# Queries' and keys' norm in an encoder kernel: the root moves beside the turning, gains multiplied straight from PSUM, query transposes and casts in two steps

## The chip, the cores and the metric

The kernel runs on one core of a Trainium2 chip. The metric is the time of one execution in device microseconds (us), median of several runs. The engines are called by the profile's names: PE (TensorE, matmuls and transposes), DVE (VectorE), ACT (ScalarE), POOL (GpSimd) and SP (which only issues DMAs here). Each engine works through its own instructions in program order, and waits where an input or a buffer isn't ready.

## The reference

Two layers of an encoder over 768 tokens (sequences of 256 and 512), width 1024. Each layer normalises its input, projects it, runs three branches side by side (windowed attention, a bidirectional mLSTM, a bidirectional state-space branch, called SSD) and merges them. The change touches the queries and keys of the attention:

```python
def rms_norm(x, g):
    y = xf * lax.rsqrt(jnp.mean(xf * xf, axis=-1, keepdims=True) + RMS_EPS)
    return (y * g.astype(jnp.float32)).astype(x.dtype)

def partial_rope(x, pos):            # turns the first 16 of a head's 64 channels
    x1 = x[..., :half]
    x2 = x[..., half:ROT_DIM]
    return jnp.concatenate([x1 * cos - x2 * sin, x2 * cos + x1 * sin, x[..., ROT_DIM:]], axis=-1)
...
proj = h @ w_in
...
aq = partial_rope(rms_norm(aq.reshape(bsz, s_len, ATT_HEADS, ATT_HEAD_DIM), q_norm_g), pos)
ak = partial_rope(rms_norm(ak.reshape(bsz, s_len, ATT_KV_HEADS, ATT_HEAD_DIM), k_norm_g), pos)
```

There are 8 query heads and 2 key heads of 64 channels.

## The kernel before

**Work and tiles.** The 768 tokens are six tiles of 128. Every fp32 operand of a large matmul is kept as two parts, a high part (rounded to the matmul's format, by an ACT cast) and a low part (the rest, by a subtraction), and a product takes three matmuls. `H` holds the normalised input in this form, transposed; `R` is an arena of such pairs, with four weight slots; `F` is an arena of plain fp32. Each layer begins with the queries (`aq`): for each tile 24 matmuls of 512 columns. Then come keys, values and gates (`akv`, 24 matmuls of 288 columns a tile), then column blocks of the other projections (128x512 and 128x256 matmuls), with the branches' own work in between. At a layer's end item `W` multiplies by the output weights, tile by tile, 48 matmuls each; its first tile needs all of `H` and eight weight pieces. In layer 0 item `W` is followed by the next layer's norm and transposes.

**Weights.** A piece of at most 128x1024 lands by DMA in a raw slot of `F`. `split_w` casts the high part on ACT, then writes the low part (`lo`) on DVE or on POOL, whichever a cost rule says would be done first; then the raw slot is free, and SP issues the next piece into it.

**The norm of a query tile** (`qk_norm`, then `q_put`). The 128x512 result stands in a PSUM bank. Before the change: ACT squares it and copies it to `F`; DVE sums the squares per head (TENSOR_REDUCE, 128x8); POOL takes the inverse root (`rstd`: TENSOR_SCALAR, then a power on 128x8); DVE multiplies by the root and then by the gains; POOL turns 16 channels of each head in four small operations; PE transposes the tile (4 transposes of 128x128); ACT casts the high part in four pieces of 64x256, DVE subtracts the low part in four. A key tile does the same with 128 columns. Tiles use three buffers in turn.

**What sets the order.** The program is written out by a planner: each chain of work (a "task") is a generator, and each `yield` ends a step. The planner has a clock model (`Clock`: a cost for each instruction, and `HOP`, the time from one engine to the next) and puts a step into the program where the model says that its inputs are ready, between groups of about six projection matmuls. So a number in the model changes where the transposes stand among the matmuls. Nothing is reordered at run time.

All engine instructions go through one helper, so they have one line, 316, in the profile; they are told apart by shapes and tiles. Line numbers below are those of the kernel before.

Of the kernel before, what the change touches and what calls it, by code (L numbers as in the profile page):

```python
# [32 lines left out]
TOK = 768  # L33
# [131 lines left out]


# [40 lines left out]
class Clock:  # L207
# [4 lines left out]
    HOP = 180.0  # L212
# [56 lines left out]
    def note(self, eng, cost, outs, ins):  # L269
        code, t, same = self.ENG[eng], 0.0 if eng == "dma" else self.free[eng], self.SAME[eng]  # L270
        acc = []
        for aps, write in ((ins, False), (outs, True)):
            for ap in aps:
                m = self.mem.get(ap.tensor.name)
                if m is None:
                    continue
                for sl in self.spans(ap):
                    acc.append((m, sl, write))
                    t = max(t, (m[0][sl] + np.where(m[1][sl] != code, self.HOP, same)).max())
                    if write:  # L280
                        t = max(t, (m[2][sl] + self.HOP * (m[3][sl] != code)).max())
        shared = eng in ("dve", "pool") and self.two(ins)
        if shared:
            t = max(t, self.port)
# [116 lines left out]
class Body:  # L401
# [295 lines left out]
    def split_w(self, slot, t, hi, lo):  # L697
        self.nc.scalar.copy(hi, t)
        yield

        at = {e: max(self.clk.free[e], self.now) + c for e, c in (("dve", 1.1 * t.shape[1]), ("pool", 2.3 * t.shape[1]))}
        g = self.nc.vector if at["dve"] <= at["pool"] else self.nc.gpsimd
        g.tensor_tensor(out=lo, in0=t, in1=hi.bitcast(F32), op=ALU.subtract)
        self.raw_back(slot)
# [183 lines left out]
    def aq_begin(self, l, _):  # L888
        s = self.S[l]
        self.finish(s["consts"])  # L890
        for g in range(2):
            s["q", g] = self.R.alloc(4 * TOK)
        s["k"] = self.R.alloc(4 * TOK)
        s["qkr"] = Ring(self.F, 3, 1024)
# [13 lines left out]
    def qk_norm(self, l, i, p, nh, goff, t):  # L908

        s, nc = self.S[l], self.nc  # L910
        st = s["qks"].next()
        n = 64 * nh
        t1, t2 = t[:, 0:n], t[:, 512:512 + n]
        a3 = t1.rearrange("p (h d) -> p h d", h=nh)
        b3 = t2.rearrange("p (h d) -> p h d", h=nh)
        nc.scalar.activation(out=t2, in_=p[:, 0:n], func=AF.Square)
# [15 lines left out]
        gp.tensor_tensor(out=b3[:, :, 0:8], in0=a3[:, :, 8:16], in1=sn0, op=ALU.mult)  # L932
        gp.tensor_tensor(out=b3[:, :, 8:16], in0=a3[:, :, 0:8], in1=sn1, op=ALU.mult)
        gp.tensor_tensor(out=a3[:, :, 0:16], in0=a3[:, :, 0:16], in1=cos, op=ALU.mult)
        gp.tensor_tensor(out=a3[:, :, 0:16], in0=a3[:, :, 0:16], in1=b3[:, :, 0:16], op=ALU.add)

    def q_put(self, l, i, p, t):
# [7 lines left out]
        parts = [(self.S[l]["q", g].ap.rearrange("p (j e t) -> p j e t", j=2, e=2),  # L945
                  b[:, 256 * g:256 * g + 256].rearrange("p (j t) -> p j t", j=2)) for g in range(2)]
# [4 lines left out]
        for q4, b3 in parts:  # L951
            for e in range(2):
                nc.vector.tensor_tensor(out=q4[half[1 - e], :, e, ts], in0=b3[half[e]], in1=q4[half[e], :, e, ts].bitcast(F32),
                                        op=ALU.subtract)
# [958 lines left out]
```

## Time and profile before

| what | value |
|---|---|
| time, median of 3 runs | 1718.99 us (1718.66 to 1720.11) |
| the profiled execution, its own time | 1719.23 us |
| its span, first to last instruction | 1717.4 us |
| mean granted TensorE clock | 0.994 of full speed |
| PE busy | 1678.1 us, 98% of the span |
| DVE busy | 916.6 us, 53% |
| ACT busy | 642.7 us, 37% |
| POOL busy | 333.5 us, 19% |
| PE's share of the chain that ended last | 87% |

The span is the time from the first instruction to the last; the run's own time has 1.8 us more around it. An engine's idle time is told with what ended it, "[1.13 <-POOL F L316]" meaning 1.13 us idle until a POOL instruction that wrote tile `F` was done. The granted clock is that at which PE was allowed to run: 1.00 is 2.4 GHz and 0.50 is 1.2 GHz.

### The profile page before, as it was taken

How to read it: one execution, taken by the hardware profiler on the slowest of the kernel's cores; microseconds unless marked ns; L12 is line 12 of the kernel's file. 1: busy time of each engine (PE TensorE's matmuls, PEld its weight loads, DVE VectorE, ACT ScalarE, POOL GpSimd, SP SyncE). 2: the span in 40 equal slices, each digit the busy share in tenths (PEclk: the TensorE clock that was granted, in tenths of full speed). 3: DMA queues.
4: the chain of work that ended last, by engine and by line, in shares of the span. 5: the costliest groups of instructions: out<-in, count | busy, mean ns of one | idle time of the engine just before them, and what ended most of it. 6: DMA issues, size and time to landing. Idle time of an engine off the chain costs nothing.

```text
span 1717.4 us, 25480 instructions
## 1 busy us (share of the span) xinstructions
PE 1678.1 (98%) x9902; PEld 1440.5 (84%) x9902; DVE 916.6 (53%) x2121; ACT 642.7 (37%) x1425; POOL 333.5 (19%) x411
## 2 busy tenths in 40 slices
PE   8899999999999999999998999999999999999999
PEld 6788888888888888888877887898888878888877
DVE  6665456454484972246346645564445859623441
ACT  5446653232332532233135466532223345222310
POOL 4513320000003112014035223100000031301230
PEclk9999999999999999999999999999999999999999
DMA  5101032321114532234211101222121145331522
GB/s 200 62 27 38 25 99 65 98 68 62 68 62 122 196 128 81 79 136 157 99 44 61 53 26 50 75 77 99 68 71 59 58 152 190 105 111 41 172 86 74
DMA packets 47881, 152.18 MB, mean 89 GB/s; under 512 B 5616, under 2 KB 6544, under 8 KB 47760
## 3 DMA queue, kind: packets, MB, share of 16 engines
q1 hardware_dynamic: 47760, 150.55, 26.1%
q8 instruction: 78, 1.28, 0.3%
q14 instruction: 43, 0.35, 0.1%
HBM read 131.51 MB, written 19.02 MB: 88 GB/s over the span
## 4 chain that ended last, share of the span: by engine, by line
PE 87%; DVE 6%; ACT 2%; POOL 2%; DMA 1%; issue 1%; SPq 0%; ACTq 0%; POOLq 0%; DVEq 0%
PE psum L316 87%; DVE F L316 3%; DVE R L316 2%; POOL F L316 2%; ACT R L316 1%; ACT F L316 1%; DMA F<-wts_dram 1%; DMA F<-csd 1%; DMA F<-cstb_dram 0%; POOL R L316 0%; SPq L316 0%; DVE H L316 0%; ACT H L316 0%; ACTq L316 0%; POOLq L316 0%
## 5 line engine op out<-in xcount | busy, mean ns | idle before, releaser
L316 PE MATMUL psum<-H,R 128*128 128x512 f32 x4800 | 889.7, 341 | 0.5 <-DVE R L316 0.5
L316 PEld LDWEIGHTS psum<-H,R 128*128 128x128 f32 x4800 | 734.7, 189 | 109.5 <-issue 7.8
L316 PE MATMUL psum<-R,H 128*128 128x512 f32 (+2 forms) x1752 | 392.2, 379 | 8.1 <-DVE R L316 4.8
L316 PEld LDWEIGHTS psum<-R,H 128*128 128x128 f32 x1752 | 310.7, 191 | 66.0 <-DVE R L316 7.4
L316 DVE TENSOR_TENSOR R<-F,R 128x1024 fp32r<-128x1024 f32 (+3 forms) x163 | 206.6, 1278 | 243.6 <-ACT R L316 242.0
L316 DVE SCALAR_TENSOR_TENSOR F<-F 128x128 f32<-128x128 f32 (+5 forms) x596 | 251.2, 469 | 76.9 <-POOL F L316 35.3
L316 POOL TENSOR_TENSOR F<-F 128x32 f32<-128x32 f32 (+9 forms) x216 | 202.4, 946 | 441.7 <-DVE F L316 243.2
L316 ACT ACTIVATE F<-F 128x128 f32<-128x128 f32 (+8 forms) x432 | 201.8, 495 | 230.6 <-DVE F L316 219.5
L316 PE MATMUL psum<-F 128*128 128x128 f32 (+5 forms) x2006 | 247.7, 287 | 27.4 <-POOL F L316 16.5
L316 PEld LDWEIGHTS psum<-F 128*128 128x128 f32 (+2 forms) x2006 | 202.3, 163 | 67.3 <-POOL F L316 21.2
L316 PE MATMUL psum<-R 128*128 128x512 f32 (+2 forms) x1344 | 247.1, 336 | 0.0
L316 ACT CAST R<-F 128x1024 fp32r<-128x1024 f32 (+3 forms) x226 | 195.0, 875 | 100.7 <-DVE F L316 50.9
L316 PEld LDWEIGHTS psum<-R 128*128 128x128 f32 x1344 | 204.2, 189 | 30.6 <-issue 2.1
L316 ACT ACTIVATE F<-psum 128x768 f32<-128x768 f32 (+2 forms) x124 | 89.0, 718 | 344.1 <-PE psum L316 276.7
L316 POOL TENSOR_SCALAR F<-F 128x256 f32<-128x256 f32 (+7 forms) x112 | 70.4, 633 | 531.4 <-ACT F L316 334.6
L316 ACT COPY F<-psum 128x256 f32<-128x256 f32 (+7 forms) x286 | 105.2, 402 | 175.9 <-PE psum L316 174.4
L316 DVE SCALAR_TENSOR_TENSOR F<-F,psum 128x768 f32<-128x768 f32 (+3 forms) x124 | 88.6, 725 | 91.1 <-PE psum L316 48.1
L316 DVE SCALAR_TENSOR_TENSOR F<-psum,F 128x128 f32<-128x128 f32 (+4 forms) x75 | 37.5, 505 | 176.9 <-PE psum L316 165.6
L316 POOL TENSOR_TENSOR R<-F,R 128x128 fp32r<-128x128 f32 (+1 forms) x63 | 60.1, 957 | 318.2 <-ACT R L316 294.0
L316 DVE TENSOR_TENSOR F<-F 128x2 f32<-128x2 f32 (+8 forms) x340 | 100.2, 305 | 32.8 <-ACT F L316 20.6
L316 DVE TENSOR_SCALAR F<-F 128x128 f32<-128x128 f32 (+5 forms) x230 | 67.4, 322 | 45.9 <-ACT F L316 22.1
L316 DVE TENSOR_TENSOR R<-psum,R 64x256 fp32r<-64x256 f32 (+2 forms) x72 | 33.5, 466 | 47.6 <-ACT R L316 46.8
(24 smaller groups left out, 282.8 us busy)
## 6 DMA issues: line engine op xcount, KB each, us to landing
F<-wts_dram SPq DMA_DIRECT2D x164, 512.0 KB, 3.6
mg<-F SPq DMA_DIRECT2D x32, 384.0 KB, 3.0
F<-mg SPq DMA_DIRECT2D x32, 384.0 KB, 4.2
F<-csd SPq DMA_DIRECT2D x32, 384.0 KB, 5.4
F<-x_dram SPq DMA_DIRECT2D x12, 512.0 KB, 7.6
F<-md SPq DMA_DIRECT2D x16, 384.0 KB, 5.5
x<-F SPq DMA_DIRECT2D x6, 512.0 KB, 2.9
F<-x SPq DMA_DIRECT2D x6, 512.0 KB, 4.0
```

The source lines that it names most:

```text
L316: r = fn(*args, **kw)
```

## The change

In `qk_norm` ACT no longer copies the tile out of PSUM. DVE multiplies it by the gains straight from PSUM into `F`, POOL turns it at once (the turning is linear and leaves the root's factor alone), DVE sums the squares meanwhile, POOL takes the root, and DVE multiplies by the root last. In `q_put` the transposes are a step of their own, the casts another, and the two blocks of queries become one of double size, so that two casts of 64x512 and two subtractions take the place of four and four. The clock model has 250 ns after PE and 170 ns after any other engine in place of 180, and the rule in `split_w` adds 2000 ns to POOL's price.

```diff
     GRAIN = 4
-    HOP = 180.0
+    HOP = 170.0
+
+    HOPS = np.array([0.0, 250.0, 170.0, 170.0, 170.0, 170.0])
...
-                    t = max(t, (m[0][sl] + np.where(m[1][sl] != code, self.HOP, same)).max())
+                    t = max(t, (m[0][sl] + np.where(m[1][sl] != code, self.HOPS[m[1][sl]], same)).max())
...
-        at = {e: max(self.clk.free[e], self.now) + c for e, c in (("dve", 1.1 * t.shape[1]), ("pool", 2.3 * t.shape[1]))}
+        at = {e: max(self.clk.free[e], self.now) + c for e, c in (("dve", 1.1 * t.shape[1]), ("pool", 2.3 * t.shape[1] + 2000.0))}
...
         nc.scalar.activation(out=t2, in_=p[:, 0:n], func=AF.Square)
-        nc.scalar.copy(t1, p[:, 0:n])
+        nc.vector.tensor_tensor(out=a3, in0=p[:, 0:n].rearrange("p (h d) -> p h d", h=nh),
+                                in1=s["cb"][:, goff:goff + 64].unsqueeze(1).to_broadcast([128, nh, 64]), op=ALU.mult)
         self.give(p)
-        yield
-        nc.vector.tensor_reduce(out=st[:, 0:nh], in_=b3, axis=AX.X, op=ALU.add)
-        yield
-        self.rstd(st[:, 8:8 + nh], st[:, 0:nh], 1.0 / 64)
-        yield
-        nc.vector.tensor_tensor(out=a3, in0=a3, in1=st[:, 8:8 + nh].unsqueeze(2).to_broadcast([128, nh, 64]), op=ALU.mult)
-        nc.vector.tensor_tensor(out=a3, in0=a3, in1=s["cb"][:, goff:goff + 64].unsqueeze(1).to_broadcast([128, nh, 64]), op=ALU.mult)
         yield
...
+        gp.tensor_tensor(out=c3[:, :, 0:8], in0=a3[:, :, 8:16], in1=sn0, op=ALU.mult)
+        gp.tensor_tensor(out=c3[:, :, 8:16], in0=a3[:, :, 0:8], in1=sn1, op=ALU.mult)
+        nc.vector.tensor_reduce(out=st[:, 0:nh], in_=b3, axis=AX.X, op=ALU.add)
         gp.tensor_tensor(out=a3[:, :, 0:16], in0=a3[:, :, 0:16], in1=cos, op=ALU.mult)
-        gp.tensor_tensor(out=a3[:, :, 0:16], in0=a3[:, :, 0:16], in1=b3[:, :, 0:16], op=ALU.add)
+        gp.tensor_tensor(out=a3[:, :, 0:16], in0=a3[:, :, 0:16], in1=c3, op=ALU.add)
+        yield
+        self.rstd(st[:, 8:8 + nh], st[:, 0:nh], 1.0 / 64)
+        yield
+        nc.vector.tensor_tensor(out=a3, in0=a3, in1=st[:, 8:8 + nh].unsqueeze(2).to_broadcast([128, nh, 64]), op=ALU.mult)
...
             self.transpose_to(b[:, 128 * j:128 * j + 128], t[:, 128 * j:128 * j + 128])
+        yield
...
-        for q4, b3 in parts:
-            for e in range(2):
-                nc.scalar.copy(q4[half[e], :, e, ts], b3[half[e]])
+        q4 = self.S[l]["qq"].ap.rearrange("p (j e t) -> p j e t", j=4, e=2)
+        b3 = b.rearrange("p (j t) -> p j t", j=4)
+        for e in range(2):
+            nc.scalar.copy(q4[half[e], :, e, ts], b3[half[e]])
```

The order of the instructions moves with it. Three places are shown, each as it stands before and then as it stands now.

DVE in the queries of layer 1, from the root of the first tile on. "F<-F 128x512" is a multiplication by root or gains, "R<-psum,R" the low parts of transposed queries, "F<-psum,F 128x512" the new multiplication from PSUM. Before:

```order
L316 TENSOR_REDUCE F<-F 128x8
L316 TENSOR_TENSOR R<-psum,R 64x2x128 x4
L316 TENSOR_TENSOR F<-F 128x512 x2
L316 TENSOR_REDUCE F<-F 128x8
L316 TENSOR_TENSOR R<-psum,R 64x2x128 x4
L316 TENSOR_TENSOR F<-F 128x512 x2
L316 TENSOR_REDUCE F<-F 128x8
L316 TENSOR_TENSOR R<-psum,R 64x2x128 x4
L316 TENSOR_TENSOR F<-F 128x512 x2
```

Now:

```order
L323 TENSOR_TENSOR F<-F 128x512
L323 TENSOR_TENSOR F<-psum,F 128x512
L323 TENSOR_REDUCE F<-F 128x8
L323 TENSOR_TENSOR R<-psum,R 64x4x128 x2
L323 TENSOR_TENSOR F<-F 128x512
L323 TENSOR_TENSOR F<-psum,F 128x512
L323 TENSOR_REDUCE F<-F 128x8
L323 TENSOR_TENSOR R<-psum,R 64x4x128 x2
L323 TENSOR_TENSOR F<-F 128x512
L323 TENSOR_TENSOR F<-psum,F 128x512
L323 TENSOR_REDUCE F<-F 128x8
```

Before, the low parts of one tile stand directly ahead of both multiplications of the next. Now a tile's multiplication by the root stands behind the gains and the sum of the same tile and behind the low parts of the tile in front.

DVE, then POOL, at the start of the output projection of layer 0. "R<-F,R 128x1024" is the low part of a weight piece, "H<-F,H 128x768" the low part of a channel block of `H`. DVE before:

```order
L316 SCALAR_TENSOR_TENSOR F<-F,psum 128x768
L316 TENSOR_TENSOR H<-F,H 128x768
L316 TENSOR_TENSOR R<-F,R 128x1024 x3
L316 TENSOR_TENSOR H<-F,H 128x768
L316 TENSOR_TENSOR R<-F,R 128x1024 x2
L316 SCALAR_TENSOR_TENSOR F<-psum,F 128x1024
```

DVE now:

```order
L323 SCALAR_TENSOR_TENSOR F<-F,psum 128x768
L323 TENSOR_TENSOR H<-F,H 128x768
L323 TENSOR_TENSOR R<-F,R 128x1024 x4
L323 TENSOR_TENSOR H<-F,H 128x768
L323 TENSOR_TENSOR R<-F,R 128x1024
L323 SCALAR_TENSOR_TENSOR F<-psum,F 128x1024
L323 TENSOR_TENSOR R<-F,R 128x1024
```

POOL before:

```order
L316 TENSOR_TENSOR F<-F 128x768 x8
L316 TENSOR_TENSOR R<-F,R 128x1024
L316 TENSOR_SCALAR F<-F 128x64
L316 TENSOR_SCALAR F<-F 128x4
L316 TENSOR_SCALAR F<-F 128x36
```

POOL now:

```order
L323 TENSOR_TENSOR F<-F 128x768 x8
L323 TENSOR_SCALAR F<-F 128x64
L323 TENSOR_SCALAR F<-F 128x4
L323 TENSOR_SCALAR F<-F 128x36
L323 TENSOR_SCALAR F<-F 128x1
```

The low part that stood on POOL in front of the next layer's constants (128x64, 128x4, 128x36) is now the fourth in a row on DVE. In the whole program POOL had 15 such low parts and has none; DVE has 164 in place of 149.

PE at the start of the program. 128x128 are transposes (the first 12 of the first row are filler matmuls), 8 for a tile of the input's norm and 4 for a query tile; 128x512 are the queries' matmuls. Before:

```order
L316 MATMUL psum<-F 128x128 x20
L316 MATMUL psum<-R,H 128x512 x18
L316 MATMUL psum<-F 128x128 x8
L316 MATMUL psum<-R,H 128x512 x6
L316 MATMUL psum<-F 128x128 x8
L316 MATMUL psum<-R,H 128x512 x18
L316 MATMUL psum<-F 128x128 x16
L316 MATMUL psum<-R,H 128x512 x18
L316 MATMUL psum<-F 128x128 x8
L316 MATMUL psum<-R,H 128x512 x12
```

Now:

```order
L323 MATMUL psum<-F 128x128 x28
L323 MATMUL psum<-R,H 128x512 x24
L323 MATMUL psum<-F 128x128 x8
L323 MATMUL psum<-R,H 128x512 x6
L323 MATMUL psum<-F 128x128 x8
L323 MATMUL psum<-R,H 128x512 x6
L323 MATMUL psum<-F 128x128 x8
L323 MATMUL psum<-R,H 128x512 x12
L323 MATMUL psum<-F 128x128 x8
L323 MATMUL psum<-R,H 128x512 x12
```

The second tile's 8 transposes stood behind 18 matmuls and now stand in front of all of them; the sixth tile's stood behind 60 matmuls and stand behind 48. Farther on, in layer 1, the transposes of query tiles stand 24 matmuls apart as before, each behind the last matmul of the next tile, where they stood in the middle of a tile.

## Rows read from the trace of the kernel before

**Rows 1.** Windows: start:end, length, busy (count) of PE, PEld, DVE, ACT, POOL; clock; DMA.

```profile
22.00:92.00 70.00, 61.49 (x357) 53.95 (x358) 48.14 (x94) 35.17 (x86) 37.28 (x77) 0.98 0.16 57
...
872.00:936.00 64.00, 54.09 (x298) 45.51 (x297) 37.77 (x70) 27.70 (x64) 31.53 (x58) 1.00 0.16 55
```

**Rows 2.** TensorE waits of the whole program, one releaser: total, times, longest.

```profile
PE psum L316 <- POOL F L316: 16.5, 10, 3.6
```

**Rows 3.** Timeline, all engines, layer 1, one query tile: start, duration, instruction, idle before.

```profile
893.75 0.66 PE L316 MATMUL psum<-F 128*128 128x128 f32 x4 [1.18 <-POOL F L316]
893.78 0.20 POOL L316 TENSOR_SCALAR F<-F 128x8 f32<-128x8 f32 x1
894.06 1.64 POOL L316 TENSOR_TENSOR F<-F 128x8 f32<-128x8 f32 x1
...
894.16 5.71 PE L316 MATMUL psum<-R,H 128*128 128x512 f32 x24
894.44 1.50 ACT L316 CAST R<-psum 64x256 fp32r<-64x256 f32 x4 [3.48 <-PE psum L316]
895.97 1.73 DVE L316 TENSOR_TENSOR R<-psum,R 64x256 fp32r<-64x256 f32 x4 [3.48 <-ACT R L316]
897.24 0.60 ACT L316 ACTIVATE F<-psum 128x512 f32<-128x512 f32 x1 [1.30 <-issue]
...
897.73 1.42 DVE L316 TENSOR_TENSOR F<-F 128x512 f32<-128x512 f32 x2
899.07 0.68 DVE L316 TENSOR_REDUCE F<-F 128x8 f32<-128x512 f32 x1
899.29 1.66 POOL L316 TENSOR_TENSOR F<-F 128x64 f32<-128x64 f32 x4 [3.60 <-DVE F L316]
...
901.00 0.66 PE L316 MATMUL psum<-F 128*128 128x128 f32 x4 [1.13 <-POOL F L316]
```

**Rows 4.** Timeline of TensorE in the keys and values of layer 0.

```profile
67.23 3.43 PE L316 MATMUL psum<-R,H 128*128 128x288 f32 x24
...
74.65 4.16 PE L316 MATMUL psum<-R,H 128*128 128x288 f32 x18
```

**Rows 5.** Timeline of layer 0 from 56.73, GpSimd and VectorE.

```profile
56.73 2.75 POOL L316 TENSOR_TENSOR F<-F 128x64 f32<-128x64 f32 x4 [3.60 <-DVE F L316]
57.10 4.60 DVE L316 TENSOR_TENSOR R<-F,R 128x864 fp32r<-128x864 f32 x4
```

**Rows 6.** Timeline, start of the output projection: layer 0, then TensorE in layer 1.

```profile
798.79 7.34 DVE L316 TENSOR_TENSOR R<-F,R 128x1024 fp32r<-128x1024 f32 x3
800.55 3.36 POOL L316 TENSOR_TENSOR R<-F,R 128x1024 fp32r<-128x1024 f32 x1
...
805.05 14.81 PE L316 MATMUL psum<-R,H 128*128 128x512 f32 x57 [1.91 <-DVE R L316]
...
1652.00 8.23 PE L316 MATMUL psum<-R,H 128*128 128x512 f32 x28 [1.91 <-DVE R L316]
```

**Rows 7.** TensorE waits in the state-space branch, 550 to 645, then 1402 to 1491.

```profile
PE psum L316 <- DVE F L316: 2.5, 2, 1.5
...
PE psum L316 <- DVE F L316: 1.3, 2, 1.2
```

**Rows 8.** Timeline of the first 34 us, layer 0.

```profile
11.32 1.07 ACT L316 ACTIVATE F<-F 128x1024 f32<-128x1024 f32 x1
...
13.92 3.60 PE L316 MATMUL psum<-R,H 128*128 128x512 f32 x8 [1.90 <-POOL R L316]
13.95 1.05 POOL L316 TENSOR_SCALAR F<-F 128x1 f32<-128x1 f32 x1
...
15.09 0.55 POOL L316 TENSOR_TENSOR F<-F 128x1 f32<-128x1 f32 x1
...
24.55 1.28 DVE L316 SCALAR_TENSOR_TENSOR F<-F 128x1024 f32<-128x1024 f32 x1
...
33.03 1.09 PE L316 MATMUL psum<-F 128*128 128x128 f32 x8
```

More of the change, by code (lines that the diff above doesn't have):

```diff
@@ L164, in free, with halves @@
         self.arena = None
+    def halves(self):
+        m = self.n // 2
+        return Block(self.arena, self.start, m, self.ap[:, 0:m]), Block(self.arena, self.start + m, self.n - m, self.ap[:, m:self.n])
 class Ring:
@@ L278, in note @@
                     acc.append((m, sl, write))
-                    t = max(t, (m[0][sl] + np.where(m[1][sl] != code, self.HOP, same)).max())
+                    t = max(t, (m[0][sl] + np.where(m[1][sl] != code, self.HOPS[m[1][sl]], same)).max())
                     if write:
-                        t = max(t, (m[2][sl] + self.HOP * (m[3][sl] != code)).max())
+                        t = max(t, (m[2][sl] + self.HOPS[m[3][sl]] * (m[3][sl] != code)).max())
         shared = eng in ("dve", "pool") and self.two(ins)
@@ L890, in aq_begin @@
         self.finish(s["consts"])
-        for g in range(2):
-            s["q", g] = self.R.alloc(4 * TOK)
+        s["qq"] = q = self.R.alloc(8 * TOK)
+        s["q", 0], s["q", 1] = q.halves()
         s["k"] = self.R.alloc(4 * TOK)
-        s["qkr"] = Ring(self.F, 3, 1024)
+        s["qkr"] = Ring(self.F, 3, 1152)
         s["qks"] = Ring(self.F, 3, 16)
@@ L912, in qk_norm @@
         n = 64 * nh
-        t1, t2 = t[:, 0:n], t[:, 512:512 + n]
+        t1, t2, t3 = t[:, 0:n], t[:, 512:512 + n], t[:, 1024:1024 + 16 * nh]
         a3 = t1.rearrange("p (h d) -> p h d", h=nh)
         b3 = t2.rearrange("p (h d) -> p h d", h=nh)
+        c3 = t3.rearrange("p (h d) -> p h d", h=nh)
         nc.scalar.activation(out=t2, in_=p[:, 0:n], func=AF.Square)
-        nc.scalar.copy(t1, p[:, 0:n])
+        nc.vector.tensor_tensor(out=a3, in0=p[:, 0:n].rearrange("p (h d) -> p h d", h=nh),
+                                in1=s["cb"][:, goff:goff + 64].unsqueeze(1).to_broadcast([128, nh, 64]), op=ALU.mult)
         self.give(p)
-        yield
-        nc.vector.tensor_reduce(out=st[:, 0:nh], in_=b3, axis=AX.X, op=ALU.add)
-        yield
-        self.rstd(st[:, 8:8 + nh], st[:, 0:nh], 1.0 / 64)
-        yield
-        nc.vector.tensor_tensor(out=a3, in0=a3, in1=st[:, 8:8 + nh].unsqueeze(2).to_broadcast([128, nh, 64]), op=ALU.mult)
-        nc.vector.tensor_tensor(out=a3, in0=a3, in1=s["cb"][:, goff:goff + 64].unsqueeze(1).to_broadcast([128, nh, 64]), op=ALU.mult)
         yield
@@ L942, in q_put @@
             self.transpose_to(b[:, 128 * j:128 * j + 128], t[:, 128 * j:128 * j + 128])
+        yield
         ts = slice(128 * i, 128 * i + 128)
         half = [slice(0, 64), slice(64, 128)]
-        parts = [(self.S[l]["q", g].ap.rearrange("p (j e t) -> p j e t", j=2, e=2),
-                  b[:, 256 * g:256 * g + 256].rearrange("p (j t) -> p j t", j=2)) for g in range(2)]
-        for q4, b3 in parts:
-            for e in range(2):
-                nc.scalar.copy(q4[half[e], :, e, ts], b3[half[e]])
+        q4 = self.S[l]["qq"].ap.rearrange("p (j e t) -> p j e t", j=4, e=2)
+        b3 = b.rearrange("p (j t) -> p j t", j=4)
+        for e in range(2):
+            nc.scalar.copy(q4[half[e], :, e, ts], b3[half[e]])
         yield
[L951 to L954, printed above, removed]
+        for e in range(2):
+            nc.vector.tensor_tensor(out=q4[half[1 - e], :, e, ts], in0=b3[half[e]], in1=q4[half[e], :, e, ts].bitcast(F32),
+                                    op=ALU.subtract)
         self.give(b)
```

2 lines of the change are left out of this document (removed).

## Prediction

> **What bounds the kernel now.** I read the page's busy shares first. TensorE works 1678.1 of 1717.4 us and the next engine, VectorE, 53% of the span, so the kernel is bound by TensorE's matmuls, and the change leaves their number and sizes as they are. What it can alter is TensorE's idle time (1717.4 − 1678.1 = 39.3 us) and the time in which TensorE runs at half clock. So the windows come second. In the stretches of queries, keys and values TensorE is busy 61.49 of 70 us in layer 0 and 54.09 of 64 in layer 1 [rows 1]: 8.5 + 9.9 = 18.4 us, nearly half of all idle time. Third, the waits: TensorE waits 16.5 us in 10 places for a tile in `F` that GpSimd writes [rows 2], and nearly all of that lies in these two stretches: the transposes of queries and keys wait for the turning.
>
> The timeline of one query tile tells why [rows 3]. From one group of transposes (893.75) to the next (901.00) pass 7.25 us, and TensorE has 0.66 + 5.71 = 6.4 us of work for them. The chain is a loop: transposes 0.66, high parts on ACT 1.50, low parts on VectorE 1.73, and behind these, because they stand later in VectorE's order, the two multiplications of the *next* tile 1.42, then the turning 1.66, then that tile's transposes. These five make 6.97 us, with the hops from engine to engine 7.25. The loop, not TensorE, sets the pace, and each round costs about 1.1 us. The next tile's root, 0.20 + 1.64 on GpSimd, lies outside the loop.
>
> **The change part by part.**
>
> *Query tiles.* The new order takes the casts out of the loop: a tile's low parts stand behind the next tile's gains and sum [the order of VectorE above], two of 64x512 instead of four of 64x256. I take 1.35 for the pair of low parts (twice the 0.68 of a 128x512 row) where 1.73 stood, and 1.2 for the casts (twice 0.60) where 1.50 stood [rows 3]; both lie beside matmuls. In place of the loop stands a line from a tile's last matmul to its transposes: hop 0.2, square on ACT 0.60, gains from PSUM, turning 1.66, root 0.20 + 1.64, multiplication by the root 0.71 (half of 1.42) [rows 3], and about 0.3 of further hops. A multiplication that reads PSUM has no row: from below 0.60 (the square reads the same 128x512 from PSUM), from above 0.87 (double of four 64x256 pieces in 1.73, which read PSUM too); nearest is the multiplication by one operand at 0.68 to 0.71, and I take 0.68. Gains come after the square in the plan, both from the same bank, so they add. Sum 0.2 + 0.60 + 0.68 + 1.66 + 0.20 + 1.64 + 0.71 + 0.3 = 6.0 us. The transposes now stand behind the next tile's 24 matmuls, so 5.71 us cover it, and the wait is about 0.3 a tile instead of about 1.1.
>
> *Where the weights' low parts interfere.* When four low parts of the next weights run on VectorE (4.60 in all, 1.15 each), the turning beside them took 2.75 instead of 1.66 [rows 5]. One tile a layer meets these: wait 0.3 + 1.1 = 1.4. The first key tile follows at the akv block's shorter groups (24 matmuls in 3.43 us [rows 4]): 0.6 in layer 0, 0.3 in layer 1. Layer 0 keeps 0.3 + 1.4 + 0.6 = 2.3 of its 8.5. There the longest wait, 3.6 [rows 2], is followed by 18 matmuls in 4.16 us where 18 × 3.43/24 = 2.57 is the full rate [rows 4]; with that wait gone these 1.6 us go too. Gain 8.5 − 2.3 + 1.6 = **7.8**. In layer 1 I leave 0.4 for weights, 0.2 for the norm of the input in front, 1.0 over the plain tiles, 1.4 and 0.3: 3.3 of 9.9. Gain **6.6**. Bounds for both together: 18.4 + 1.6 = 20 if nothing waits, 4.7 if every tile waits as before (see rivals).
>
> *Rule of split_w.* With 2000 ns on its price GpSimd gets none of the 15 low parts, VectorE gets them. At the start of item `W` in layer 0 GpSimd's piece ran from 800.55 for 3.36 us, to 803.9, and the three on VectorE beside it took 7.34, 2.4 each, until 806.1; TensorE, waiting 1.91 us for VectorE, began at 805.05 with 57 matmuls in 14.81 us [rows 6]. Alone on VectorE a piece needs about 1.25 (between the 1.15 of 864 columns [rows 5] and that scaled to 1024, 1.36). GpSimd is done with its earlier work by 800.55, so the first ends at about 801.6 and the others at 802.9, 804.1 and 805.3. TensorE is free at 803.1 (805.05 − 1.91) and needs the second: no wait. At full rate 57 × 5.71/24 = 13.57, so 1.24 of half clock go as well: **3.15**. Layer 1 has the same place: 1.91, and 28 matmuls in 8.23 where 6.67 is the full rate: **3.5**. Bounds 0 (another piece is late in its turn) and these. The 15 low parts cost VectorE 15 × 1.25 = 19 us of its 800 idle ones. They are covered as long as a piece is ready before TensorE's next weights are; where that cover is gone, a piece late by one place costs up to 1.25.
>
> *State-space branch.* TensorE waits 2.5 + 1.3 = 3.8 us there for VectorE's scans' operands [rows 7]. The new clock model moves the heads' small matmuls by up to 64 matmuls' length. Following the new order by hand I find none that must wait, but VectorE is busy nearly throughout; I take **2.8**, bounds 0 and 3.8.
>
> *Start.* The eight transposes of the second tile's norm now stand ahead of all 24 matmuls of the first query tile [the order of TensorE above]. Their tile's square ends at about 12.4 (11.32 + 1.07), the root's first step took 1.05 beside a low part, the next 0.55, the normalising multiplication 1.28 [rows 8]: together 15.3. Until then TensorE has nothing to do, and its first 512-column matmul comes at about 16.4, after eight transposes (1.09); before, it ran eight from 13.92 on and had a few done earlier. A stretch at half clock follows, as there (8 in 3.60, 0.45 each against 0.238). Carried on to the sixth tile's transposes, with 1.25 of waiting at the fourth's, I reach at about 37.0 the work that ended at 34.1 (33.03 + 1.09 [rows 8]): **−2.9**, bounds −5 and 0.
>
> *Elsewhere.* The plan of everything moves a little, and transposes of other branches may come early: I take **−1.5**, bounds −3 and 0, from the waits outside these places, which hold 39.3 − 18.4 − 3.8 (item `W`) − 3.8 = 13 us already.
>
> Sum: 7.8 + 6.6 + 3.15 + 3.5 + 2.8 − 2.9 − 1.5 = 19.5. The profiled execution took 1719.23 us (span 1717.4 and 1.8 around it), 0.24 above the median. 1719.2 − 19.5 = 1699.7; against the median 1699.5.
>
> **A rule beside the rows.** The turning ran beside a TENSOR_REDUCE of VectorE (899.07 to 899.75) and took 1.66; beside weight low parts, which read both operands from SBUF, 2.75 [rows 3, 5]. The Trainium skill, page "SBUF — State Buffer", section "Who interferes with whom", says that a VectorE instruction with two SBUF inputs contends with a GpSimd instruction that reads SBUF, and that one with at most one such input (outside its two-port modes) does not. These rows agree with it. By that rule the new multiplication from PSUM holds nobody, since the tile itself comes from PSUM, while the multiplication by the root does, at a time when GpSimd has nothing to turn, so that the sum stays. It speaks against the third part: 15 more low parts with two SBUF inputs on VectorE can hold the turning more often; the rival below prices that.
>
> **The rivals.**
>
> *Slower: VectorE holds GpSimd in every tile.* Turning and root now both lie on the path. If low parts of weights, moved to VectorE, run beside each of them, the turning loses 2.75 − 1.66 = 1.1 [rows 3, 5], the root's first step 1.05 − 0.20 = 0.85 [rows 3, 8] and the power about as much: 2.8 a tile, in 12 tiles 33.6 us, hence 1699.7 + 33.6 = 1733. It decides for slower from 19.5 / 12 = 1.6 us a tile on. For it speaks that 15 parts move; against it that a layer has only four weight pieces in this stretch for six query tiles, and that they come in one row.
>
> *The wait stays.* The model's hop between other engines is now shorter (170 for 180), so a chain is believed ready earlier than before, and root and turning in series are longer than the loop's share was. If transposes are put where the line of 6.0 us isn't covered, the twelve tiles wait 1.15 each as now: 13.8 instead of the 4.1 (2.3 + 3.3, less the 1.5 that weights and keys take) in my sum, 9.7 more: 1709.4. For it: cover 5.7 against a line of 6.0, which is thin. Against it: the order shows each tile's transposes a whole tile later.
>
> *More gain.* No new waits elsewhere (1.5), nothing lost at the start (2.9) and a wait-free line (about 3): 19.5 + 7.4 = 27, so 1692.
>
> *No change.* The moved plan loses elsewhere what the stages win, about 19 us; it would need more waits than the whole rest of the program has (13 us).
>
> **How the numbers follow.** My case 0.62, the wait that stays 0.17, more gain 0.08, slower 0.08, no change 0.05. All but the last two are faster by over 0.2% (3.4 us, about what a measurement of this kernel can tell from no change): 0.87 faster, 0.05 the same, 0.08 slower. My own case reaches from 1694 to 1705 by the bounds of its terms. The range 1690 to 1711 takes in the wait that stays and most of the larger gain and leaves out 1733 and no change, about 1.5 in 10.
>
> **What would show it.** Right: waits of TensorE for GpSimd's `F` fall from 16.5 us to about 5; idle time per stretch from 8.5 and 9.9 to 2 to 4; at the start of item `W` no wait for VectorE, and a full clock behind it; TensorE's first 512-column matmul at about 16; 164 low parts of weights on VectorE and none on GpSimd; the gains from PSUM near 0.7. Wrong: query transposes that wait 1 us or more in every tile; a turning at 2.7 in most; new waits for VectorE's low parts in the projections' blocks; more than 5 us lost at the start.

## The result, and the profile after

The changed kernel takes 1699.7 us (median of 4 runs, 1698.3 to 1700.66) against 1719.55 us (4 runs, 1718.66 to 1720.64): a ratio of 0.9884, 95% interval 0.9867 to 0.9901. From the page of the profiled execution, its span and the busy times:

```profile
span 1696.5 us, 25376 instructions
...
PE 1669.7 (98%) x9902; PEld 1435.2 (85%) x9902; DVE 909.3 (54%) x2112; ACT 629.3 (37%) x1377; POOL 299.7 (18%) x396
```

The span is 20.9 us shorter than the 1717.4 of before. It has two halves: idle time of TensorE fell from 39.3 to 26.8 us (1696.5 − 1669.7), 12.5 less, and its busy time from 1678.1 to 1669.7, 8.4 less, at the same number of matmuls. Most of the second half is time at half clock that is gone. The waits of TensorE over the whole program, with total, times and longest (answering to [rows 2]):

```profile
PE psum L323 <- DVE F L323: 13.9, 12, 5.5
PE psum L323 <- ACT F L323: 6.2, 6, 1.2
```

Nothing waits for GpSimd's `F` any more, where 16.5 us did. The waits for ACT are six of the keys' transposes; the largest single wait, 5.5, is the start. The windows of the changed kernel that answer to [rows 1] (start and end, length, TensorE's busy time; the granted clock is the third number from the end):

```profile
0.00:35.70 35.70, 26.46 (x134) 22.85 (x135) 23.01 (x30) 20.09 (x32) 13.65 (x28) 0.90 0.65 241
22.00:92.00 70.00, 65.20 (x386) 56.41 (x385) 47.41 (x90) 29.63 (x61) 38.15 (x77) 1.00 0.16 56
859.00:927.00 68.00, 62.74 (x357) 53.40 (x356) 40.84 (x75) 25.80 (x54) 35.84 (x74) 1.00 0.18 59
```

Idle time from 22 to 92 is 4.8 us in place of 8.5, and that includes 0.7 that still belongs to the start; the query and key stretch of layer 1, now 859 to 927, has 5.3 in place of 9.9. The half clock that went is seen in windows of the kernel before, the first of them the stretch up to the sixth tile's transposes:

```profile
0.00:34.20 34.20, 27.25 (x134) 22.17 (x134) 21.50 (x25) 20.25 (x33) 15.47 (x23) 0.95 0.68 251
74.00:79.00 5.00, 4.76 (x26) 4.77 (x26) 2.57 (x7) 2.21 (x7) 3.20 (x13) 0.66 0.01 3
612.00:622.00 10.00, 8.47 (x38) 7.57 (x38) 4.97 (x14) 0.90 (x2) 0.10 (x1) 0.66 0.32 118
803.00:813.00 10.00, 8.09 (x29) 6.44 (x29) 7.59 (x6) 2.10 (x2) 0.92 (x1) 0.83 0.77 257
1650.00:1660.00 10.00, 8.09 (x29) 6.50 (x29) 5.24 (x5) 0.00 (x0) 0.86 (x1) 0.83 0.00 0
```

Behind the wait of 3.58 the granted clock is 0.66, in the state-space branch 0.66, at both starts of item `W` 0.83. Busy time times what is missing from 1.00 gives 1.6, 2.9, 1.4 and 1.4 us, 7.3 in all. The clock of the changed kernel is 1.00 in all places that answer to these; below 1.00 it is only from 10 to 20 us, where it is 0.66 against 0.83 before and costs 0.5 us more. The clock so accounts for about 6.8 of the 8.4 us. A second execution of the changed kernel (after_again, below) has 1671.2 us of busy time, so about as much as the rest lies between two executions of one kernel.

The query tile of layer 1 that answers to [rows 3], timeline of all engines:

```profile
883.88 0.66 PE L323 MATMUL psum<-F 128*128 128x128 f32 x4
883.98 0.60 ACT L323 ACTIVATE F<-psum 128x512 f32<-128x512 f32 x1 [4.32 <-issue]
...
884.29 5.72 PE L323 MATMUL psum<-R,H 128*128 128x512 f32 x24
...
884.61 0.69 DVE L323 TENSOR_TENSOR F<-psum,F 128x512 f32<-128x512 f32 x1 [0.78 <-ACT F L323]
885.22 0.68 DVE L323 TENSOR_REDUCE F<-F 128x8 f32<-128x512 f32 x1
885.38 1.68 POOL L323 TENSOR_TENSOR F<-F 128x64 f32<-128x64 f32 x4 [2.28 <-DVE F L323]
885.92 1.39 DVE L323 TENSOR_TENSOR R<-psum,R 64x512 fp32r<-64x512 f32 x2
887.15 0.20 POOL L323 TENSOR_SCALAR F<-F 128x8 f32<-128x8 f32 x1
887.43 1.65 POOL L323 TENSOR_TENSOR F<-F 128x8 f32<-128x8 f32 x1
889.11 0.69 DVE L323 TENSOR_TENSOR F<-F 128x512 f32<-128x512 f32 x1 [1.79 <-POOL F L323]
...
889.86 0.66 PE L323 MATMUL psum<-F 128*128 128x128 f32 x4
```

From one transposes to the next it is 5.98 us, where it was 7.25. The line is all there in the order of the change, from the square (883.98) through gains (0.69), turning, root and last multiplication to 889.86, 5.9 us long, and the wait ahead of these transposes is too short to be listed.

At item `W` of layer 0 (answering to [rows 6]) TensorE runs on without a wait, while four low parts follow one another on VectorE:

```profile
786.66 15.61 PE L323 MATMUL psum<-R,H 128*128 128x512 f32 x68
...
788.60 6.29 DVE L323 TENSOR_TENSOR R<-F,R 128x1024 fp32r<-128x1024 f32 x4
```

At the start (answering to [rows 8]):

```profile
15.03 1.97 PE L323 MATMUL psum<-F 128*128 128x128 f32 x8 [5.45 <-DVE F L323]
...
16.65 6.38 PE L323 MATMUL psum<-R,H 128*128 128x512 f32 x24
```

### The profile page after: what moved, and what is told of

It reads as the page before. It is cut to its first block, busy times and chain, and to the rows that moved or that the text cites. A ratio compares the mean times of both kernels' runs of the same rounds, so it can differ in the third digit from the quotient of the medians.

```text
span 1696.5 us, 25376 instructions
## 1 busy us (share of the span) xinstructions
PE 1669.7 (98%) x9902; PEld 1435.2 (85%) x9902; DVE 909.3 (54%) x2112; ACT 629.3 (37%) x1377; POOL 299.7 (18%) x396
## 4 chain that ended last, share of the span: by engine, by line
PE 87%; POOL 4%; DVE 3%; issue 3%; DMA 2%; ACT 1%; SPq 0%; POOLq 0%; ACTq 0%; DVEq 0%
PE psum L323 87%; POOL F L323 4%; DVE F L323 2%; DMA F<-csd 1%; DVE R L323 1%; DMA F<-wts_dram 1%; ACT F L323 0%; DMA F<-cstb_dram 0%; ACT R L323 0%; SPq L323 0%; ACT H L323 0%; DVE H L323 0%; POOLq L323 0%; ACTq L323 0%; DVEq L323 0%
## 5 line engine op out<-in xcount | busy, mean ns | idle before, releaser
L323 PE MATMUL psum<-R,H 128*128 128x512 f32 (+2 forms) x1752 | 386.2, 375 | 0.9 <-DVE F L323 0.5
L323 PEld LDWEIGHTS psum<-R,H 128*128 128x128 f32 x1752 | 306.1, 188 | 54.9 <-DVE R L323 1.4
L323 DVE TENSOR_TENSOR R<-F,R 128x1024 fp32r<-128x1024 f32 (+3 forms) x178 | 220.0, 1244 | 237.2 <-ACT R L323 235.2
L323 DVE SCALAR_TENSOR_TENSOR F<-F 128x128 f32<-128x128 f32 (+5 forms) x596 | 244.4, 456 | 76.8 <-POOL F L323 33.8
L323 POOL TENSOR_TENSOR F<-F 128x512 f32<-128x512 f32 (+9 forms) x216 | 203.3, 951 | 430.8 <-DVE F L323 255.0
L323 ACT COPY F<-psum 128x256 f32<-128x256 f32 (+6 forms) x262 | 95.1, 400 | 176.6 <-PE psum L323 168.8
L323 DVE TENSOR_TENSOR F<-F 128x2 f32<-128x2 f32 (+8 forms) x316 | 86.3, 283 | 42.4 <-POOL F L323 22.7
L323 DVE TENSOR_SCALAR F<-F 128x128 f32<-128x128 f32 (+5 forms) x230 | 63.0, 302 | 41.0 <-ACT F L323 22.2
L323 DVE TENSOR_TENSOR F<-F,psum 128x129 f32<-128x129 f32 (+2 forms) x104 | 35.8, 376 | 36.4 <-ACT F L323 25.6
L323 DVE CUSTOM_DVE_ANT_0 F<-psum,F 128x256 f32<-128x256 f32 (+1 forms) x96 | 40.9, 464 | 10.4 <-PE psum L323 9.1
```

The source lines that it names most:

```text
L323: r = fn(*args, **kw)
```

## The experiments

The change has four parts, and the experiments take them apart: the **order** of the norm (`qk_norm`), the **split** of transposes and casts (`q_put`, with the double block), the **price** in `split_w`, and the **model** (`HOP`, `HOPS`). Every ratio is against the kernel before in runs on the same chip. The table gives, from each kernel's profiled execution, the sum of TensorE's waits in the query and key stretches of layer 0 and layer 1.

| kernel | order | split | price | model | waits, us | ratio (95%) |
|---|---|---|---|---|---|---|
| before | – | – | – | – | 8.5 + 9.9 | 1 |
| p_only | – | – | yes | – | 8.2 + 7.4 | 0.9983 (0.9971 to 0.9996) |
| n_only | yes | – | – | – | 3.9 + 13.0 | 1.0027 (1.0015 to 1.0039) |
| n_p | yes | – | yes | – | 9.4 + 12.1 | 1.0040 (1.0028 to 1.0053) |
| no_q | yes | – | yes | yes | 5.0 + 7.9 | 0.9897 (0.9880 to 0.9915) |
| nq | yes | yes | – | – | 3.5 + 4.9 | 0.9953 (0.9936 to 0.9969) |
| no_p | yes | yes | – | yes | 4.4 + 5.0 | 0.9930 (0.9917 to 0.9942) |
| no_h | yes | yes | yes | – | 3.2 + 5.3 | 0.9916 (0.9900 to 0.9931) |
| no_n | – | yes | yes | yes | 5.2 + 4.2 | 0.9906 (0.9886 to 0.9925) |
| after | yes | yes | yes | yes | 3.8 + 5.3 | 0.9884 (0.9867 to 0.9901) |
| late_p | yes | yes | later | yes | 4.2 + 4.9 | 0.9884 (0.9866 to 0.9902) |
| key_twice | yes | yes | yes | yes | 5.0 + 6.8 | 0.9883 (0.9866 to 0.9899) |
| keys_old | queries | yes | yes | yes | 1.5 + 4.9 | 0.9880 (0.9861 to 0.9899) |

**The changed kernel once more** (after_again), as a control, no edit.

> The changed kernel once more, beside the others of this call and on their chip: a control. About 0.988 of the kernel before.

Measured 1697.25 us, 0.9867 (0.9851 to 0.9884), with the same waits as in the first profile within 0.1 us in the two stretches.

**The price alone** (p_only), the kernel before with:

```diff
-("pool", 2.3 * t.shape[1]))}
+("pool", 2.3 * t.shape[1] + 2000.0))}
```

> The kernel before with GpSimd's price in split_w alone (2000 ns more). Theory A (each part pays at its own place): item W loses its two waits of 1.91 us and the half clock behind them, some 6.0 us, the start loses 1.6 us since its transposes move as in the change, query and key stretches keep their waits (idle 8.5 and 9.9 us, within 2 us each): 1719.5 - 4.5 = 1715 us, 1712 to 1717. Rival B (GpSimd, freed of weights, turns sooner, and that is where the query stretches' gain came from): idle time in these two stretches falls to about 5 each and the time to 1708 or less.

Measured 1716.8 us against 1719.8, in theory A's range. Both waits of item `W` are gone, the query stretches wait much as before (8.2 and 7.4, still for GpSimd): rival B is out. The median gains less than the 4.5 us forecast. In the profiled execution a weight's low part on VectorE comes 3.83 us late at 1011 us, with half clock behind it (see the model, below). That execution is the fastest of twelve (1711.8 to 1720.2 us) and its span is 7.4 us shorter than that of the kernel before all the same, so what makes the median smaller is not shown.

**Without the price** (no_p), the changed kernel with that line as before.

> The changed kernel without the price. Theory A: the waits of 1.91 us at both starts of item W come back with their half clock (+6.0 us), the start gets its 1.6 us back, query and key stretches stay at an idle time of 4 to 5 us each: 1699.7 + 4.4 = 1704 us, 1701 to 1707. Rival B: the stretches' idle time goes back to 8 us or more each, 1711 or above.

Measured 1708.6. The waits of 1.91 at `W` are back, the query stretches keep their short waits, as theory A has it, but the time lies above its range: the start did not get its 1.6 us back, it became worse. Besides, TensorE waits 2.12 us for ACT at 562 us, which it does in no other kernel. At the start, the sixth tile's transposes end at 39.5 us, where the changed kernel has that and as many matmuls done at 35.7 and the kernel before at 34.1. VectorE, GpSimd and TensorE in no_p:

```profile
26.46 0.55 POOL L323 TENSOR_TENSOR F<-F 128x1 f32<-128x1 f32 x1
...
27.43 0.69 DVE L323 TENSOR_TENSOR F<-psum,F 128x512 f32<-128x512 f32 x1 [3.98 <-ACT F L323]
28.04 1.28 DVE L323 TENSOR_TENSOR H<-psum,H 128x512 fp32r<-128x512 f32 x2
...
29.23 3.79 DVE L323 SCALAR_TENSOR_TENSOR F<-F 128x1024 f32<-128x1024 f32 x3
...
30.57 1.10 PE L323 MATMUL psum<-F 128*128 128x128 f32 x8 [2.08 <-DVE F L323]
```

The normalisation of an input tile (the first of three from 29.23) had its root by 27.0. It stands behind the first query tile's gains (27.43), the new multiplication from PSUM, for which VectorE had been idle 3.98 us until ACT's square was done, and behind two low parts. In the kernel before, the first instruction of VectorE that needs a query tile is the sum (28.71), and it stands behind this normalisation (26.54). TensorE waits 2.08 us for it, with half clock behind. With the price the second tile's transposes stand ahead of the queries' matmuls, the first query tile is finished later, and its gains (25.11 in the changed kernel) stand behind the normalisations of the next two tiles.

**The price after the start only** (late_p):

```diff
+("pool", 2.3 * t.shape[1] + (2000.0 if self.now > 40000.0 else 0.0)))}
```

> The changed kernel, with the 2000 ns on GpSimd's price only after the first 40 us of the plan's clock; before that GpSimd gets low parts as in the kernel before. It parts the price's two places. If it pays at the start too, with the new norm: the sixth tile's transposes end at 39 us instead of 36, while item W has no wait: 3 to 4 us more than the changed kernel, 0.989 to 0.991. Rival (the price pays at item W alone and costs at the start, as predicted): 1.5 us less than the changed kernel, 0.986 to 0.988.

Measured 1700.6 us, between the two theories' ratios. By place it is as the first theory says: the wait of 2.07 at 31 us and its half clock are there, the sixth tile's transposes end at 39.6 us (35.7 for as much work in the changed kernel), and there is no wait at `W`. By time it can't be told from the changed kernel, whose two intervals span the same; its profiled execution is 4.8 us longer (1701.3 us of span), but it is the slowest of five beside the fastest of four. That the price pays at the start is shown by the place, not by the medians.

**The order of the norm alone** (n_only), the kernel before with the change's `qk_norm` and its ring of 1152 columns.

> The kernel before with the new order of the norm alone (gains from PSUM, turning, root last); casts and transposes in one step as before, four casts and four low parts a tile. Theory A: the low parts of a tile no longer stand in front of the next tile's turning, so the loop is broken by this part alone: idle time in the two stretches 18.4 to about 9 us, 1719.5 - 9 = 1710 us, 1707 to 1713. Rival D (the split of transposes and casts is needed, since the longer line of 6 us is not covered where the transposes stand in mid-tile): waits for VectorE of about 1 us in each query tile, idle time 15 us or more, 1716 or above.

Measured 1725.1: slower. Layer 0 behaves as theory A says (3.9), layer 1 as rival D says and worse (13.0, four waits of 1.4 to 3.8). A tile of layer 1 in n_only:

```profile
899.12 0.69 DVE L316 TENSOR_TENSOR F<-psum,F 128x512 f32<-128x512 f32 x1 [3.68 <-ACT F L316]
899.84 1.73 DVE L316 TENSOR_TENSOR R<-psum,R 64x256 fp32r<-64x256 f32 x4
899.89 1.68 POOL L316 TENSOR_TENSOR F<-F 128x64 f32<-128x64 f32 x4 [5.17 <-DVE F L316]
901.58 0.69 DVE L316 TENSOR_REDUCE F<-F 128x8 f32<-128x512 f32 x1
902.36 0.20 POOL L316 TENSOR_SCALAR F<-F 128x8 f32<-128x8 f32 x1 [0.79 <-DVE F L316]
...
904.32 0.69 DVE L316 TENSOR_TENSOR F<-F 128x512 f32<-128x512 f32 x1 [2.05 <-POOL F L316]
...
905.07 0.66 PE L316 MATMUL psum<-F 128*128 128x128 f32 x4 [2.65 <-DVE F L316]
```

The previous tile's four low parts (899.84) still stand between a tile's gains and its sum, so the sum ends at 902.3, the root follows, and the transposes, which stand in mid-tile as before, wait 2.65. The loop over low parts is still there; it only goes through the sum and the root now instead of the two multiplications and the turning.

**Order and price** (n_p), nothing else of the change.

> The kernel before with the norm's new order and GpSimd's price, nothing else. Theory E: the parts interact at the start. The norm alone puts the new multiplication from PSUM, which waits for the square, in front of the input norm's work on VectorE (wait of 2.07 us and half clock); with the price the second tile's transposes come earlier and this wait goes, so the sixth tile's transposes end by 36 us instead of 37.9; item W gains its 6 us; layer 1's query stretch stays as bad as with the norm alone (12 us idle). In sum 0.996 to 0.999. Rival (the parts add): 1.0027 x 0.9983 = 1.001, and the start at 38 us.

Measured 1726.3, the slowest of all. The start is as theory E says, 35.6 us for the first 60 matmuls of 512 columns against 37.1 in n_only. But layer 0's stretch now waits 9.4 us too, and at 1025 a low part comes 3.71 late. The forecast of 0.996 to 0.999 failed. A tile of layer 0 now shows the same order as layer 1 of n_only: gains (48.91), the previous tile's four low parts (49.64), the sum (51.38), and transposes that wait 2.67 (54.86). What moved the plan there stays open.

**Without the split** (no_q): the changed kernel with `q_put` and the blocks of before.

```diff
         for j in range(4):
             self.transpose_to(b[:, 128 * j:128 * j + 128], t[:, 128 * j:128 * j + 128])
-        yield
...
+        for q4, b3 in parts:
+            for e in range(2):
+                nc.scalar.copy(q4[half[e], :, e, ts], b3[half[e]])
```

> The changed kernel with the casts as before: transposes and four casts in one step, four low parts, two blocks. Theory E (transposes as a step of their own are what keeps a tile's sum of squares in front of the low parts on VectorE and its transposes behind the next tile's matmuls): layer 1 goes back to idle times like those with the norm alone (waits of 1.4 to 3.8 us, 10 us or more in the stretch, against 5.3), some half clock too, in all 5 to 9 us more: 0.991 to 0.994 of before. Rival F (the split saves only two casts and two low parts off the path): within 2 us of the changed kernel.

Measured 1702.5 beside 1697.25 for the changed kernel in the same series: 5.2 us slower, the low end of theory E and outside rival F, with a ratio just below E's range. Its query tiles wait 0.4 to 1.3 each, not 1.4 to 3.8, and the two stretches 3.8 us more than in the changed kernel, at full clock. The low parts still stand between a tile's gains and its sum (49.89, 50.61 and 52.35 in one tile). The split matters, but with the model's numbers its lack costs far less than in n_p, which is this kernel without them.

**Order and split, without price and model** (nq).

> The kernel before with the norm's new order and the split casts, without price and clock model. Theory E' (the line of 6 us must be covered, and either the split or the clock model puts the transposes a whole tile later; the norm alone has neither): query tiles wait little, idle time near 5 us a stretch, but item W waits twice (1.91 each) and the start loses 4 to 5 us against the kernel before as the norm alone did: 0.993 to 0.995. Rival (the clock model is what the new norm needs): waits of 1.3 to 2.7 us a tile as with the norm alone, 1.000 to 1.003.

Measured 0.9953, just above the upper end of theory E'. The stretches wait as little as in the changed kernel; `W` waits 1.91 twice, the start 2.08. So price and model are not what the query tiles need.

**Without the model's numbers** (no_h): `HOP` 180 for all engines.

> The changed kernel with the old clock model (180 ns from every engine). Theory A: the gain comes from the order of the norm's operations, the model's numbers matter little: 1699.7, within 3 us, query tiles without waits. Rival C (where the transposes stand decides, and the model's 250 ns after TensorE puts them there): query transposes come up to six matmuls earlier, wait about 1 us in each of 12 tiles, 1708 to 1712 us.

Measured 1706.0, in the gap between the theories. Of the query tiles only two wait, both in layer 1 (1.42, where the changed kernel waits 1.07, and 0.24), so rival C is out. The profiled execution, the fastest of five and 3.2 us longer than the changed kernel's, points to a third reason. VectorE and TensorE in layer 1:

```profile
997.47 1.21 DVE L323 TENSOR_TENSOR R<-F,R 128x1024 fp32r<-128x1024 f32 x1
...
998.74 4.38 PE L323 MATMUL psum<-R,H 128*128 128x512 f32 x11 [3.71 <-DVE R L323]
```

A weight's low part is late on VectorE behind the branches' small operations, and TensorE waits 3.71 us, 1.5 more at half clock. Such a wait of 2.3 to 3.8 us stands at about 155 or 1000 us in p_only, n_p, no_h, no_n and keys_old, which all have the price, and in none of the kernels without it. The changed kernel, no_q, late_p and key_twice have the price and no such wait.

**Without the order** (no_n): the changed kernel with the root first and the turning last, as before.

> The changed kernel with the old order of the norm (root first, both multiplications from F, then the turning); split casts, price and clock model as changed. Theory A (the old order makes a loop over the tiles that is longer than TensorE's work, wherever the transposes stand): query transposes wait for GpSimd about 1 us a tile again, 8 us or more of idle time in each stretch, 0.993 to 0.997 of before. Rival C (split and clock model alone place the transposes late enough): idle time 5 us or less a stretch, 0.988 to 0.990.

Measured 1703.5, ratio 0.9906. This is the run that decides: theory A, 8 us or more in each stretch, is wrong. With the old order the two stretches wait 5.2 + 4.2 us, in sum about what the changed kernel waits. The sum hides a shift. The waits of TensorE for GpSimd in no_n's two stretches, all of them at query tiles:

```profile
PE psum L323 <- POOL F L323: 3.7, 4, 1.6
...
PE psum L323 <- POOL F L323: 2.6, 2, 2.1
```

That is 6.3 us, where the changed kernel's query tiles wait 2.5 (0.61, 1.07 and 0.82). Its keys wait 6.2 and those of no_n 2.6. So the new order, with the split there, still saves 3.8 us at the query tiles and loses 3.6 at the keys. TensorE, VectorE and GpSimd in no_n:

```profile
43.27 0.66 PE L323 MATMUL psum<-F 128*128 128x128 f32 x4 [0.48 <-POOL F L323]
...
43.68 5.73 PE L323 MATMUL psum<-R,H 128*128 128x512 f32 x24
...
45.25 1.42 DVE L323 TENSOR_TENSOR F<-F 128x512 f32<-128x512 f32 x2 [3.25 <-POOL F L323]
...
46.70 1.39 DVE L323 TENSOR_TENSOR R<-psum,R 64x512 fp32r<-64x512 f32 x2
46.81 1.69 POOL L323 TENSOR_TENSOR F<-F 128x64 f32<-128x64 f32 x4 [1.60 <-DVE F L323]
...
49.24 0.60 PE L323 MATMUL psum<-F 128*128 128x128 f32 x4
```

The two multiplications of a tile (45.25) now stand *ahead* of the previous tile's low parts (46.70), whose casts have become a step of their own, and the transposes stand 24 matmuls apart, behind the next tile (49.24, no wait listed). At the first of these tiles (43.27) the low parts stood in front once more, and it waits 0.48. The ratio of no_n is not clear of the changed kernel's, as the intervals overlap; its profiled execution is 5.2 us longer (1701.7 us of span). Places for that are a low part 2.26 late at 159 us with 1.5 us of half clock behind it, and half clock behind the longest of the query tiles' waits (granted clock 0.83 from 909 to 919 us).

**Keys without ACT's copy** (key_twice): the multiplication by the root writes the doubled key tile.

```diff
+        if twice:
+            nc.vector.tensor_tensor(out=t[:, 512:768].rearrange("p (v e d) -> p v e d", v=2, e=2),
+                                    in0=a3.unsqueeze(2).to_broadcast([128, 2, 2, 64]),
...
-        nc.scalar.copy(t[:, 512:768].rearrange("p (v e d) -> p v e d", v=2, e=2),
```

> The changed kernel, but the keys' multiplication by the root writes the doubled tile itself and ACT's copy of it falls away (output unchanged). Theory G (the keys' waits of 0.7 to 1.25 us come from a line that is one copy too long): the line is 0.45 us shorter, six waits of 6.2 us in all fall to about 3.5, 2.7 us less than the changed kernel. Rival H (the copy is not the cause, the multiplication by the root stands behind queries' low parts on VectorE or the planner puts the transposes earlier by as much): the waits stay at 5 us or more, no change within 1 us.

Measured 1699.6 against 1697.25 beside it: no gain. The transposes now wait for VectorE (layer 0, query tiles included):

```profile
PE psum L323 <- DVE F L323: 5.0, 6, 1.7
```

Rival H holds: with a shorter line the plan puts the transposes earlier. In the changed kernel the second key tile is held by something else anyway (VectorE, ACT, TensorE):

```profile
69.96 1.84 DVE L323 TENSOR_TENSOR R<-psum,R 64x512 fp32r<-64x512 f32 x3 [1.40 <-ACT R L323]
...
71.73 0.28 DVE L323 TENSOR_TENSOR F<-F 128x128 f32<-128x128 f32 x1
...
72.31 0.40 ACT L323 COPY F<-F 128x256 f32<-128x256 f32 x1
...
72.76 0.44 PE L323 MATMUL psum<-F 128*128 128x128 f32 x2 [1.04 <-ACT F L323]
```

Its multiplication by the root (71.73) stands behind low parts of queries (69.96, 1.84), then the copy, then a wait of 1.04.

**Keys in the old order** (keys_old): `k_put` calls the norm of before, queries the new one.

> The changed kernel with the old order of the norm for the keys alone (output unchanged). Theory K (in the new order the keys' turning and root stand one behind the other on GpSimd, behind the queries' in program order, and the planner takes them for ready 1 us too early): the keys' waits for ACT fall from 6 us to 2, about 3 to 4 us less than the changed kernel, 0.985 to 0.986. Rival (the keys wait because the last queries' root and low parts, and weights' low parts, hold GpSimd and VectorE in front of them, whatever the keys' order): the waits stay at 5 us or more, 0.987 to 0.990.

Measured 1700.4. In layer 0 what is left of the stretch's waits is two query tiles; the keys' are gone:

```profile
PE psum L323 <- DVE F L323: 1.5, 2, 0.9
```

In layer 1 the keys' fall from 3.0 to 1.8. So theory K holds for the waits (6.2 to 1.8), but the last query tile of each layer now waits 0.9 and 0.8, and a low part is late by 2.27 at 155 us: the time can't be told from the changed kernel's. None of the variants beats it.

## Why the prediction was right, and where it was not

The time came out as forecast, 1699.7 against 1699.5, but that it came so close is luck, since errors of the terms cancelled. The terms, measured as idle time plus half clock in the two profiled executions (at the start, as the time of the same 134 matmuls):

| term | predicted | measured | from |
|---|---|---|---|
| layer 0, queries and keys | 7.8 | 6.3 | waits 8.5 to 3.8, half clock 1.6 |
| layer 1, queries and keys | 6.6 | 4.6 | 9.9 to 5.3 |
| `W`, layer 0 | 3.15 | 2.6 | 1.91 gone, next norm's wait 0.35 to 1.02, half clock 1.4 |
| `W`, layer 1 | 3.5 | 3.3 | 1.91 and half clock 1.4 |
| state-space branch | 2.8 | 3.5 | waits 3.8 to 3.2, half clock 2.9 |
| start | −2.9 | −1.5 | windows of 34.2 and 35.7 us |
| elsewhere | −1.5 | +2.1 | the rest of 20.9 |

**Query tiles: the cost was right, the cause was half wrong.** The line of 6.0 us measured 5.9, the gains from PSUM 0.69 (0.68 taken), the transposes' cover 24 matmuls; the plain tiles wait less than the 0.3 each that I took, and the tile beside the weights' low parts 0.6 and 0.8 instead of 1.4. There the power of the root was held (2.47 us at 54.28 in place of 1.65), not the turning, which took 1.69 (52.23). Only the first tile of layer 1 waits 1.07, which I had not priced. But the prediction's step that the *new order of the norm* takes the casts and low parts out of the loop fails: alone it leaves the loop and costs 0.27% (n_only), and without it the waits sum to as little (no_n), though the query tiles' part of them is 3.8 us larger. The runs point to the split instead, which makes transposes, casts and low parts separate steps: in the eight kernels with it, the two stretches' waits sum to 6.4 to 11.8 us, in the five without it to 12.9 to 21.5. Three pairs of kernels differ in it alone: n_only and nq (16.9 to 8.4), n_p and no_h (21.5 to 8.5), no_q and the changed kernel (12.9 to 9.1). The split also makes casts and low parts fewer and shorter (1.18 for 1.50, 1.39 for 1.73), and no run parts this from the separate steps. With the new order it is enough without price and model (nq). With the old order it was tried only together with both; the price alone changes little there (p_only), the model alone was not tried, so what part of no_n's short waits is the model's stays open.

**Keys: a size that was too small.** I gave the first key tile of each layer 0.6 and 0.3. Three in each layer wait about 1 us, 6.2 in all. The prediction also read the old waits wrong where it took keys among the transposes that wait for the turning: all ten waits for GpSimd are at query tiles, and the keys waited in the kernel before only this:

```profile
PE psum L316 <- ACT F L316: 1.5, 3, 0.9
```

So the change makes the keys 4.7 us worse. At one of them the rows show the last multiplication behind queries' low parts on VectorE; with the old order, where that multiplication comes before the turning, 1.8 of the 6.2 are left (keys_old). The keys wait 5.3 us more than priced; the rest waits 1.8 less than priced, and so the two stretches fall 3.5 us short. Their idle time, 4.8 and 5.3, stayed above the 2 to 4 that was to show the prediction right.

**Item `W`** went as worked out: no wait, full clock. The four low parts took 6.29 us (1.57 each, 1.25 taken), and still were early enough.

**The start** began as forecast (transposes at 15.03 against 15.3, matmuls from 16.65 against 16.4) and lost less: as much work as the kernel before has done at 34.1 us is done at 35.7, not at 37.0. The half clock there cost little (the 24 matmuls from 16.65 took 6.38, where 5.71 is the full rate; the prediction names no sum for it), and the wait ahead of a later tile's transposes is 0.70 (28.25) in place of 1.25. That the price does it is half of the story: with the new order the start without the price is worse still (no_p, nq and n_only wait 2.07 to 2.08 there). This interaction I had not seen.

**State-space branch:** the sum is near, the reason isn't. Following the order by hand I had found none that must wait, but two waits stay in each layer, 1.7 us in layer 0 and 1.5 in layer 1 (TensorE's waits from 546 to 641 and from 1388 to 1476):

```profile
PE psum L323 <- DVE F L323: 1.7, 2, 1.4
```

```profile
PE psum L323 <- DVE F L323: 1.5, 2, 1.2
```

What went is half clock. Over the kernels the waits there vary without one part deciding it, so this gain belongs to the plan as it fell out; its cause stays open.

**Elsewhere** I expected new waits; small ones went instead: the listed waits outside the places above sum to 2.4 us in the kernel before and 0.5 in the changed one. The risk was real: five of the nine kernels with the price have a low part 2.3 to 3.8 us late, and the changed kernel is among the other four. That is why removing a part, the model's numbers too, can cost 5 us at a place that the part doesn't touch.

**The rivals.** VectorE holding GpSimd in every tile: the turning took 1.68 (885.38) beside the sum and the low parts, which read PSUM, so no. The rule of the Trainium skill, page "SBUF — State Buffer", section "Who interferes with whom", that a VectorE instruction with at most one SBUF input, outside its two-port modes, leaves GpSimd alone, agrees with this row. The wait that stays: it is what the order alone would have brought.

## What to carry to other kernels

A chain that goes round through several tiles is broken where one tile's late work stands in front of the next tile's early work on an engine that runs in order; look first at which step puts it there, since cutting a step in two may do more than a shorter chain. An instruction that reads PSUM ties its engine to the matmuls: whatever stands behind it waits with it, here the input norm at the start (in no_p VectorE was idle 3.98 us ahead of the gains, and TensorE waited 2.08 behind). When a planner writes the order, the parts of a change don't add; take single parts away from the whole, not only add them to the old kernel, and compare waits by place before times.

## What was not expected of the hardware

The same wait is not always followed by half clock. Item `W` of no_p waits 1.91 us for VectorE at both places, as the kernel before does, but the windows behind the two show the full granted clock, where the kernel before had 0.83:

```profile
799.00:809.00 10.00, 8.09 (x36) 6.37 (x35) 7.94 (x6) 2.62 (x3) 1.26 (x1) 1.00 0.76 264
1642.00:1652.00 10.00, 8.09 (x36) 6.35 (x36) 5.58 (x5) 0.00 (x0) 1.20 (x1) 1.00 0.13 47
```

In nq the clock is full behind the first wait of 1.91 (1.00 from 799 to 809 us) and 0.83 behind the second (1645 to 1655).

And of the 20.9 us saved, idle time is 12.5 and half clock about 6.8: in this kernel the half clock was worth about half as much as the waits.
